# Attention scores by four products: the queries' rest against the rounded keys alone, in two 64-row tiles of TensorE

## The chip, the core and the metric

One Trainium2 chip; the kernel runs on one of its cores. The metric is the device time of one execution in microseconds; the runs of the kernel before and of the changed kernel are compared by their medians.

## What is computed

One step of a streaming encoder: an input projection, a state-space branch, a GLU, a banded attention and an output projection. The change is in the attention of the prompt's 2048 positions, 8 heads of 64 dimensions. The reference, cut to this:

```python
s = jnp.einsum('bnqhd,bnkhd->bnhqk', chunks(q), kb).astype(jnp.float32) * (HEAD_DIM ** -0.5)
bias = _rel_bias(rel_table, dist)
s = jnp.where(valid[None, :, None, None, :], s + bias[None, None], NEG_INF)
p = jax.nn.softmax(s, axis=-1).astype(v.dtype)
o = jnp.einsum('bnhqk,bnkhd->bnqhd', p, vb)
```

`q` and `k` are RMS-normalised per head. A chunk of 64 queries sees its own 64 keys and the 512 before them.

## The kernel before

TensorE multiplies values that are rounded to its fp32r format, so every number is carried as two parts: `hi`, the rounded value, and `lo`, the rest (`x - hi`, rounded again). A product of two numbers then needs several products of parts.

The program is one foreground (the input projection, then the GLU, then the output projection, all through `mm3`, lines 180 to 185: three matmuls of 512 columns for each 128 rows of the contraction) into which a background is woven (the state-space branch, the decode attention, then `attention`, lines 1093 to 1325). `run` (line 1517) adds up the costs that the foreground yields, multiplies them by `ratio`, and lets the background go on until its own yielded costs are paid. The order of all instructions is thus fixed when the program is built. It doesn't look at times, only at the yielded numbers and at counters.

**Keys and queries** are made in the input projection (`ev_norm`, lines 263 to 310). `turn` transposes a tile of 128 positions into PSUM (`pt`, 128 partitions = 2 heads x 64 dimensions, 4 pairs of heads, 128 positions). ScalarE writes `hi` (line 297), VectorE `lo` (line 298), both into `o[:, m, x, t]` with x = 0 for `hi` and 1 for `lo`. Two DMAs store `o` into the DRAM tensor `kt_d` (keys) or `qt_d` (queries).

**Scores.** `attention` goes through 16 units (a group `G` of 512 queries and a pair of heads `m`), each with 2 heads `s` and 4 blocks `a` of 128 queries: 128 steps. A unit loads keys into `KS[n]`: partitions 0 to 63 hold `hi` of a key's 64 dimensions, partitions 64 to 127 hold `lo` of the same key. `Q[n, 0]` holds the queries' `hi` twice, on both halves of the partitions, and `Q[n, 1]` their `lo` twice. So one matmul over 128 partitions adds q_hi k_hi + q_hi k_lo, and a second one q_lo k_hi + q_lo k_lo. `qk` (lines 1155 to 1176) does this over the `w` keys that the block sees: 640 keys in two halves of 320 (two PSUM banks, so four matmuls, 96 of the steps), and in the first group (`G` = 0, 32 of the steps) 128, 256, 384 or 512 keys in one bank by two matmuls. The PSUM tile `s` exists once; the next `qk` waits until it has been read.

```python
for x2 in range(2):
    nc.tensor.matmul(ps_s[:, bank, 0:wp], Q[n, x2][:, s, 128 * a:128 * a + 128],
                     KS[n][:, s, c0:c0 + wp], start=(x2 == 0), stop=(x2 == 1))
```

VectorE then adds the bias and takes each row's minimum in one instruction (line 1174; signs are turned, so the minimum serves the softmax), `soft` takes the exponential on ScalarE (line 1183), `tr` transposes the result by up to five TensorE transposes (line 1194), which ScalarE and VectorE split again into `pth` and `ptl` (lines 1201, 1202), and `pv` multiplies by the values (line 1212). A step is `qk` of block i, then foreground, then `tr` of block i - 1, then foreground, then `soft` of block i.

Elsewhere the kernel already uses parts of TensorE's array: the decode attention places matmuls in column tiles of 32 (lines 1009, 1012, 1051), and the state-space branch has transposes of 16 partitions (line 727), which the program places in a row tile of 32 rows and 128 columns. The transposes of line 1035 are placed in a tile of 128 rows and 32 columns.

Of the kernel before, what the change touches and what calls it, by code (L numbers as in the profile page):

```python
# [7 lines left out]
F32 = mybir.dt.float32  # L8
F32R = mybir.dt.float32r
I32 = mybir.dt.int32  # L10
AF = mybir.ActivationFunctionType
OP = mybir.AluOpType
# [19 lines left out]
def fv(ap):  # L32
    return ap.bitcast(F32)


def ap_of(t, offset, pat):
    return bass.AP(tensor=t.tensor, offset=t.offset + offset, ap=pat)


class Build:  # L40
# [146 lines left out]
    def inproj(self):  # L187
        nc, I, tc = self.nc, self.I, self.tc
        wp, hp, ev = self.wp, self.hp, self.ev
# [47 lines left out]
        def store(n, dst, src):  # L237
            self.defer(n, lambda: nc.sync.dma_start(dst, src))
# [24 lines left out]
        def ev_norm(g, t, z):  # L263
            r = self.rstd[:, t:t + 1]
            zs = ev.tile([128, 512], F32, tag="zs", name="zs")
            sq = ev.tile([128, 512], F32, tag="sq", name="sq", bufs=1)
            s8 = ev.tile([128, 8], F32, tag="s8", name="s8")
            nc.scalar.activation(out=sq, in_=z, func=AF.Square, scale=r)
            nc.scalar.activation(out=zs, in_=z, func=AF.Copy, scale=r)
            z3 = zs.rearrange("p (h d) -> p h d", h=8)  # L270

            def power():
                nc.vector.tensor_reduce(s8, sq.rearrange("p (h d) -> p h d", h=8), axis=AX.X, op=OP.add)  # L273
                nc.gpsimd.tensor_scalar(s8, s8, 1.0 / 64, EPS, op0=OP.mult, op1=OP.add)  # L274
                nc.gpsimd.tensor_tensor(out=s8, in0=s8, in1=self.nhalf, op=OP.pow)  # L275

            def scale():
                nc.vector.tensor_mul(z3, z3, s8[:, :, None].to_broadcast([128, 8, 64]))
                if g == "k" and t >= 12:
                    o = ev.tile([128, 512], F32, tag="plain", name="plain")  # L280
                    nc.gpsimd.tensor_tensor(out=o.rearrange("p (h d) -> p h d", h=8), in0=z3,
                                            in1=self.kgrow[:, None, :].to_broadcast([128, 8, 64]), op=OP.mult)
                    store(4, self.O["kp"][(t - 12) * 128:(t - 11) * 128] if t < 16 else self.O["ks"], o)

            def turn():
                pt = self.pst.tile([128, 4, 128], F32, tag="tr", name="pt")
                for m in range(4):
                    nc.tensor.transpose(pt[:, m], zs[:, m * 128:(m + 1) * 128], self.ident)  # L288
                gcol = (self.kg2 if g == "k" else self.qg2)[:, 0:1]
                o = ev.tile([128, 4, 2, 128], F32R, tag="kt", name="kt", bufs=1)  # L290
                if t == 16:
                    o = fv(o).rearrange("p m x t -> p (m x t)")[:, 0:512].rearrange("p (m t) -> p m t", m=4)
                    nc.scalar.activation(out=o, in_=pt, func=AF.Copy, scale=gcol)
                    store(2, self.ksd if g == "k" else self.qsd, o)
                    return
                hi, lo = o[:, :, 0], o[:, :, 1]
                nc.scalar.activation(out=hi, in_=pt, func=AF.Copy, scale=gcol)
                self.defer(2, lambda: nc.vector.scalar_tensor_tensor(lo, pt, gcol, fv(hi), op0=OP.mult,
                                                                     op1=OP.subtract))
                for h in range(2):  # L300
                    if g == "k":
                        dst = ap_of(self.kt_d, 2048 * h + 128 * t, [[4096, 64], [64 * 4096, 8], [1, 128]])
                    else:
                        dst = ap_of(self.qt_d, 64 * 1024 * (t // 4) + 512 * h + 128 * (t % 4),
                                    [[1024, 64], [4 * 64 * 1024, 8], [1, 128]])
                    store(4 + h, dst, fv(o)[64 * h:64 * h + 64].rearrange("p m x t -> p (m x) t"))

            self.defer(2, power)
            self.defer(self.T_SCALE, scale)
            self.defer(self.T_TURN, turn)  # L310

        def ev_silu(g, t, z):
# [29 lines left out]
        n = 0  # L342
# [39 lines left out]
        for ps in range(3):  # L382
            for ti, t in enumerate(TILES):
# [5 lines left out]
                for gi in range(2):  # L389
                    g = passes[ps][gi]  # L390
# [702 lines left out]
    def attention(self):  # L1093
        nc = self.nc
        st = ExitStack()
        p = self.pool(st, "att", side="right", bufs=2)
        ps = self.pool(st, "attps", side="right", space=PSUM)
        KS, Q, VB, BI, GA = {}, {}, {}, {}, {}
# [51 lines left out]
        def span(x):  # L1150

            n, s, a = x
            return a if units[n][1] else 4

        def qk(x):
            n, s, a = x
            j0 = span(x)
            w = (a + 5 - j0) * 128
            parts = [(0, w)] if w <= 512 else [(0, 320), (320, 320)]
            ps_s = ps.tile([128, 2, 512], F32, tag="s", name="s")  # L1160
            for bank, (c, wp) in enumerate(parts):
                c0 = 128 * j0 + c
                for x2 in range(2):
                    nc.tensor.matmul(ps_s[:, bank, 0:wp], Q[n, x2][:, s, 128 * a:128 * a + 128],  # L1164
                                     KS[n][:, s, c0:c0 + wp], start=(x2 == 0), stop=(x2 == 1))
            sn = p.tile([128, 640], F32, tag="sn", name="sn")
            mn = p.tile([128, 1], F32, tag="mn", name="mn")
            b = BI[2 * n + s][:, 640 - w:640]
            if len(parts) == 2:
                o, i0, i1 = (sn.rearrange("p (a k) -> p a k", a=2), ps_s[:, :, 0:320],  # L1170
                             b.rearrange("p (a k) -> p a k", a=2))
            else:
                o, i0, i1 = sn[:, 0:w], ps_s[:, 0, 0:w], b
            nc.vector.tensor_tensor_reduce(out=o, in0=i0, in1=i1, scale=1.0, scalar=3e38, op0=OP.add, op1=OP.min,  # L1174
                                           accum_out=mn)
            S[x] = sn, mn, w

        def soft(x):
# [93 lines left out]
        for i in range(N + 6):  # L1272
            self.att_left = N + 6 - i
            if i < N:
                x = subs[i]
                while not self.flags.get(("ga", 4 * units[x[0]][1] + 3)):
                    yield None
                qk(x)
                yield self.W_QT * SL
                flush()  # L1280
            done = i >= 2 and subs[i - 2][2] == 3 if i - 2 < N else False
            if done:
                n, s, a = subs[i - 2]
# [28 lines left out]
            if i < N:  # L1312
                n, r = x[0], i % 8
# [287 lines left out]
```

## Time and profile before

| | |
|---|---|
| median of 3 runs | 1228.08 us (1226.01 to 1228.82) |
| the profiled execution's own time | 1228.56 us |
| its span, first to last instruction | 1226.8 us |
| TensorE matmul busy | 1195.7 us (97%) |
| VectorE, ScalarE, GpSimd busy | 742.5, 598.2, 365.5 us |
| the score matmuls (line 1164), 448 of them | 87.5 us busy |
| VectorE's bias and minimum (line 1174), 128 of them | 93.3 us busy |

The matmul column of the profile counts an instruction from its start to its modelled end, and the next one starts before that end. So what a matmul takes in a stream is read from start to start, or from the chain that ended last, which follows ends. The weight load of a matmul (PEld) is an instruction of its own.

### The profile page before, as it was taken

The page shows a single profiled execution, that of the slowest core. Times are in us where ns is not written, and L with a number is a line of the kernel's source. Part 1 is how long each engine was busy: PE and PEld are TensorE (multiplying, and loading weights), DVE is VectorE, ACT ScalarE, POOL GpSimd, SP SyncE. Part 2 cuts the span into 40 slices and gives each one's busy share as a digit, 9 for nine tenths or more (in the row PEclk, how much of TensorE's full clock was granted, in tenths as well). Part 3 has the DMA queues.
Part 4 walks back from the last instruction along what each step waited for, and adds up shares of the span by engine and source line. Part 5 has one row for each costly group of instructions (what it writes and reads, how often), then busy time and mean ns, then how long its engine had stood idle before and what let it go on. Part 6 is the DMA issues. An engine that isn't in the chain of part 4 may idle for free.

```text
span 1226.8 us, 18936 instructions
## 1 busy us (share of the span) xinstructions
PE 1195.7 (97%) x6687; PEld 986.6 (80%) x6687; DVE 742.5 (61%) x1391; ACT 598.2 (49%) x1159; POOL 365.5 (30%) x455
## 2 busy tenths in 40 slices
PE   8999999999999998999999999999999999999998
PEld 6788888778788876887777878888888888888876
DVE  5233565968999898985444455565565555555511
ACT  6344355356666657553232356565554454554410
POOL 2432243457777645540000011111112121121120
PEclk9899999999999999999999999999999999999999
DMA  8776556655555557433895688886877778767242
GB/s 253 230 225 203 175 160 204 203 143 137 135 141 135 153 155 233 125 101 88 257 379 184 194 245 243 257 274 195 219 206 225 210 228 248 205 203 225 66 149 100
DMA packets 190119, 236.58 MB, mean 193 GB/s; under 512 B 58136, under 2 KB 122656, under 8 KB 189000
## 3 DMA queue, kind: packets, MB, share of 16 engines
q1 hardware_dynamic: 189016, 232.15, 63.3%
q0 software_dynamic: 864, 3.21, 0.9%
q8 instruction: 53, 0.87, 0.3%
q14 instruction: 42, 0.34, 0.1%
q10 hardware_dynamic: 144, 0.00, 0.0%
HBM read 169.48 MB, written 67.80 MB: 193 GB/s over the span
## 4 chain that ended last, share of the span: by engine, by line
PE 77%; DVE 6%; DMA 6%; ACT 3%; POOL 3%; issue 2%; SPq 1%; DVEq 0%; ACTq 0%; POOLq 0%
PE z L183 18%; PE z L185 18%; PE z L184 18%; PE o L1212 6%; PE pt L1194 5%; PE s L1164 5%; DMA wraw<-in_w_in_dram 3%; PE pt L288 1%; PE o L1051 1%; PE y L837 1%; PE y L836 1%; SPq L695 1%; PE v L765 1%; POOL s L275 1%; ACT whi L149 1%
## 5 line engine op out<-in xcount | busy, mean ns | idle before, releaser
L183 PE MATMUL z<-whi,hhi 128*128 128x512 f32 x816 | 340.1, 417 | 4.5 <-ACT hhi L222 2.8
L184 PE MATMUL z<-wlo,hhi 128*128 128x512 f32 x816 | 321.9, 395 | 2.0 <-DVE wlo L150 1.8
L185 PE MATMUL z<-whi,hlo 128*128 128x512 f32 x816 | 321.5, 394 | 0.0
L183 PEld LDWEIGHTS z<-whi,hhi 128*128 128x128 f32 x816 | 154.7, 190 | 41.5 <-issue 5.1
L184 PEld LDWEIGHTS z<-wlo,hhi 128*128 128x128 f32 x816 | 155.1, 190 | 34.8 <-DVE wlo L150 6.3
L185 PEld LDWEIGHTS z<-whi,hlo 128*128 128x128 f32 x816 | 154.5, 189 | 34.3 <-DVE hlo L225 0.8
L1201 ACT ACTIVATE pth<-pt 128x640 fp32r<-128x640 f32 (+4 forms) x128 | 81.8, 639 | 128.9 <-PE pt L1194 89.4
L1202 DVE TENSOR_TENSOR ptl<-pt,pth 128x640 fp32r<-128x640 f32 (+4 forms) x128 | 94.6, 739 | 60.8 <-ACT pth L1201 59.9
L183 PE MATMUL z<-whi,mh 128*128 128x512 f32 x272 | 113.7, 418 | 0.0
L1109 POOL MEMSET bias<- 64x64 f32 x32 | 4.7, 146 | 360.0 <-DMA bias<-tl_d 248.8
L1183 ACT ACTIVATE sn<-sn,mn 128x640 f32<-128x640 f32 (+4 forms) x128 | 97.0, 758 | 29.4 <-DVE mn L1174 29.4
L185 PE MATMUL z<-whi,ml 128*128 128x512 f32 x272 | 107.1, 394 | 0.5 <-POOL ml L1409 0.5
L184 PE MATMUL z<-wlo,mh 128*128 128x512 f32 x272 | 106.7, 392 | 0.0
L1174 DVE CUSTOM_DVE_ANT_0 sn<-s,bias 128x640 f32<-128x640 f32 (+4 forms) x128 | 93.3, 729 | 11.0 <-PE s L1164 10.5
L1164 PE MATMUL s<-ks,q 128*128 128x320 f32 (+1 forms) x448 | 87.5, 311 | 0.0
L1194 PE MATMUL pt<-ident,sn 128*128 128x128 f32 x560 | 82.9, 274 | 4.5 <-ACT sn L1183 2.4
L1164 PEld LDWEIGHTS s<-ks,q 128*128 128x128 f32 x448 | 74.7, 188 | 11.1 <-DVE mn L1174 1.2
L1194 PEld LDWEIGHTS pt<-ident,sn 128*128 128x128 f32 x560 | 65.0, 140 | 23.1 <-ACT sn L1183 10.7
L225 DVE TENSOR_TENSOR hlo<-xraw,hhi 128x1024 fp32r<-128x1024 f32 x49 | 60.9, 1243 | 23.3 <-ACT hhi L222 23.2
L274 POOL TENSOR_SCALAR s<-s 128x8 f32<-128x8 f32 x34 | 14.8, 435 | 184.6 <-DVE s L273 184.0
L1222 DVE TENSOR_TENSOR ot<-o,tmp 64x512 f32<-64x512 f32 x32 | 22.0, 688 | 74.5 <-ACT tmp L1220 74.5
L275 POOL TENSOR_TENSOR s<-s,nhalf 128x8 f32<-128x8 f32 x34 | 61.0, 1795 | 2.9
(268 smaller groups left out, 2165.6 us busy)
## 6 DMA issues: line engine op xcount, KB each, us to landing
xraw<-in_xT_dram SPq DMA_DIRECT2D x49, 512.0 KB, 4.2
q<-qt_d SPq DMA_DIRECT2D x64, 256.0 KB, 9.6
ks<-kt_d SPq DMA_DIRECT2D x28, 512.0 KB, 5.2
vhl<-vp_d SPq DMA_DIRECT2D x28, 512.0 KB, 6.6
wraw<-in_w_in_dram SPq DMA_DIRECT2D x48, 256.0 KB, 4.1
bias<-tl_d SPq DMA_DIRECT2D x32, 320.0 KB, 6.1
mt<-mt_d SPq DMA_DIRECT2D x17, 512.0 KB, 6.4
x<-in_x_dram SPq DMA_DIRECT2D x34, 256.0 KB, 5.6
```

Source lines behind the costliest of these rows:

```text
L183: mm(z, a, whi, start=first, stop=False)
L184: mm(z, a, wlo, start=False, stop=False)
L185: mm(z, b, whi, start=False, stop=last)
L225: nc.vector.tensor_sub(lo, raw, fv(hi))
L275: nc.gpsimd.tensor_tensor(out=s8, in0=s8, in1=self.nhalf, op=OP.pow)
L1164: nc.tensor.matmul(ps_s[:, bank, 0:wp], Q[n, x2][:, s, 128 * a:128 * a + 128], KS[n][:, s, c0:c0 + wp], start=(x2 == 0), stop=(x2 == 1))
L1174: nc.vector.tensor_tensor_reduce(out=o, in0=i0, in1=i1, scale=1.0, scalar=3e38, op0=OP.add, op1=OP.min, accum_out=mn)
L1183: nc.scalar.activation(out=sn[:, 0:w], in_=sn[:, 0:w], func=AF.Exp, scale=-1.0, bias=mn, accum_out=SUM[n][:, a, s:s + 1])
L1194: nc.tensor.transpose(t[:, k], pr[:, 128 * k:128 * k + 128], self.ident)
L1201: nc.scalar.activation(out=h, in_=t[:, 0:w], func=AF.Copy)
L1202: post.append(lambda: nc.vector.tensor_tensor(out=l, in0=t[:, 0:w], in1=fv(h), op=OP.subtract))
L1212: nc.tensor.matmul(o[:, a0:a1], VB[n][:, j, s, :], t[:, 3 * a0 + j + a0:4 * (a1 - 1) + j + 1:4], start=(y == 0 and j == 4), stop=(y == 1 a ...
```

## The change

`qk` leaves out the product q_lo k_lo. It multiplies q_hi by all 128 partitions of the keys as before, and q_lo by the 64 partitions that hold k_hi. To have two such half products at once, the keys are stacked differently: of every 128 keys, the first 64 have `hi` on partitions 0 to 63 and `lo` on 64 to 127, and the other 64 the other way round. The first kind (y = 0) goes to PSUM bank 0, the second (y = 1) to bank 1. The two half products use row tiles at row 0 and at row 64, 128 columns wide. The bias and the minimum are now one VectorE instruction for each bank, and the second starts from the first one's minimum. In `turn`, ScalarE writes the new layout in one instruction, and VectorE writes the keys' `lo` in two.

```diff
+                if g == "k":
+                    o4 = o.rearrange("p m x (y t) -> p m (x y) t", y=2)
+                    hi, lo, src = o4[:, :, 0::3], o4[:, :, 2:0:-1], pt.rearrange("p m (y t) -> p m y t", y=2)
+                nc.scalar.activation(out=hi, in_=src, func=AF.Copy, scale=gcol)
+                for y in ((0, 1) if g == "k" else (slice(0, 128),)):
+                    self.defer(2, lambda y=y: nc.vector.scalar_tensor_tensor(
+                        lo[:, :, y], src[:, :, y], gcol, fv(hi[:, :, y]), op0=OP.mult, op1=OP.subtract))
...
-            parts = [(0, w)] if w <= 512 else [(0, 320), (320, 320)]
-            for bank, (c, wp) in enumerate(parts):
-                c0 = 128 * j0 + c
-                for x2 in range(2):
-                    nc.tensor.matmul(ps_s[:, bank, 0:wp], Q[n, x2][:, s, 128 * a:128 * a + 128],
-                                     KS[n][:, s, c0:c0 + wp], start=(x2 == 0), stop=(x2 == 1))
+            q0, q1 = (Q[n, x2][:, s, 128 * a:128 * a + 128] for x2 in range(2))
+            ks = KS[n][:, s, 128 * j0:128 * j0 + w].rearrange("p (j y t) -> p y j t", y=2, t=64)
+            for y in range(2):
+                nc.tensor.matmul(ps_s[:, y, 0:w // 2], q0, ks[:, y], start=True, stop=False)
+            for y in range(2):
+                r = slice(64 * y, 64 * y + 64)
+                nc.tensor.matmul(ps_s[:, y, 0:w // 2], q1[r], ks[r, y], start=False, stop=True,
+                                 tile_position=(64 * y, 0))
...
-            nc.vector.tensor_tensor_reduce(out=o, in0=i0, in1=i1, scale=1.0, scalar=3e38, op0=OP.add, op1=OP.min,
-                                           accum_out=mn)
+            m = 3e38
+            for y in range(2):
+                nc.vector.tensor_tensor_reduce(out=o[:, y], in0=ps_s[:, y, 0:w // 2].rearrange("p (j t) -> p j t", t=64),
+                                               in1=i1[:, y], scale=1.0, scalar=m, op0=OP.add, op1=OP.min,
+                                               accum_out=mn[:, y:y + 1])
+                m = mn[:, 0:1]
+            mn = mn[:, 1:2]
```

On TensorE, in a step of 640 keys in the second half of the attention (`z` is the foreground's output projection, `s` the scores, `ks` the keys, `q` the two parts of the queries), there stood before:

```order
L184 MATMUL z<-wlo,mh 128x512
L185 MATMUL z<-whi,ml 128x512
L1164 MATMUL s<-ks,q_10225 128x320
L1164 MATMUL s<-ks,q_10259 128x320
L1164 MATMUL s<-ks,q_10225 128x320
L1164 MATMUL s<-ks,q_10259 128x320
L183 MATMUL z<-whi,mh 128x512
L184 MATMUL z<-wlo,mh 128x512
```

and now:

```order
L184 MATMUL z<-wlo,mh 128x512
L185 MATMUL z<-whi,ml 128x512
L1171 MATMUL s<-ks,q_10072 128x320 x2
L1174 MATMUL s<-ks,q_10105 128x320 x2
L183 MATMUL z<-whi,mh 128x512
L184 MATMUL z<-wlo,mh 128x512
```

Four matmuls stay four (line 1174's two are the row tiles), and what surrounds them is the same; steps of 128 to 512 keys have four now and had two. On VectorE, in a step of 640 keys while the GLU is the foreground (`ptl` is the split of an earlier block's weights, `ms` a GLU output, `mo` the gated attention output), there stood before:

```order
L1202 TENSOR_TENSOR ptl<-pt,pth 128x640
L1174 ISA sn,mn<-s,bias 128x640
L1174 ISA mn 128x1
L1391 SCALAR_TENSOR_TENSOR ms<-th,z 128x512
L1247 TENSOR_TENSOR mo<-ot,pt 128x256
```

and now:

```order
L1213 TENSOR_TENSOR ptl<-pt,pth 128x640
L1182 ISA sn,mn<-s,bias 128x5x64
L1182 ISA mn 128x1
L1182 ISA sn,mn<-s,bias,mn 128x5x64
L1182 ISA mn 128x1
L1402 SCALAR_TENSOR_TENSOR ms<-th,z 128x512
L1258 TENSOR_TENSOR mo<-ot,pt 128x256
```

One instruction with its reading of the accumulator became two, at the same place; the second reads what the first wrote.

## Rows read from the trace of the kernel before

**Rows 1.** The page: span, busy time by engine, engines on the chain.
```profile
span 1226.8 us, 18936 instructions
...
PE 77%; DVE 6%; DMA 6%; ACT 3%; POOL 3%; issue 2%; SPq 1%; DVEq 0%; ACTq 0%; POOLq 0%
```
**Rows 2.** Waits of PE, 700 to 1165 us: total us, times, longest.
```profile
PE pt L1194 <- ACT sn L1183: 2.4, 4, 1.6
PE pt L1194 <- DVE ptl L1202: 2.1, 5, 0.8
```
**Rows 3.** Windows: busy us (instructions) of PE, PEld, DVE, ACT, POOL; clock, DMA.
```profile
900.00:1000.00 100.00, 100.00 (x587) 87.30 (x586) 55.56 (x109) 51.05 (x95) 17.77 (x21) 1.00 0.73 215
```
**Rows 4.** Chain that ended last, 1048 to 1050.2 us: start, us, what.
```profile
1049.01 0.58 PE s L1164 x4
1049.59 0.23 PE z L183
```
**Rows 5.** Timeline of PE, 1048.7 to 1049.7 us: start, us, engine, line.
```profile
1048.62 0.39 PE L185 MATMUL z<-whi,ml 128*128 128x512 f32 x1
```
**Rows 6.** Timeline of PEld, the same stretch.
```profile
1048.62 0.70 PEld L1164 LDWEIGHTS s<-ks,q 128*128 128x128 f32 x4
1049.28 0.19 PEld L183 LDWEIGHTS z<-whi,mh 128*128 128x128 f32 x1
```
**Rows 7.** Timeline of PE, 259.2 to 260.4 us, around transposes in row tiles.
```profile
259.06 0.40 PE L185 MATMUL z<-whi,hlo 128*128 128x512 f32 x1
259.38 0.42 PE L727 MATMUL ut<-ident,P 16*128 16x16 f32 x4
259.73 0.50 PE L183 MATMUL z<-whi,hhi 128*128 128x512 f32 x1
260.07 0.39 PE L184 MATMUL z<-wlo,hhi 128*128 128x512 f32 x1
```
**Rows 8.** Timeline of PEld, the same stretch.
```profile
259.38 0.32 PEld L727 LDWEIGHTS ut<-ident,P 16*128 16x128 f32 x4 [0.36 <-ACT P L713]
259.73 0.19 PEld L183 LDWEIGHTS z<-whi,hhi 128*128 128x128 f32 x1
259.84 0.19 PEld L184 LDWEIGHTS z<-wlo,hhi 128*128 128x128 f32 x1
```
**Rows 9.** Timeline of PE, 638.4 to 640.4 us, around column tiles.
```profile
638.38 0.40 PE L185 MATMUL z<-whi,hlo 128*128 128x512 f32 x1
638.71 1.07 PE L1009 MATMUL s<-kc,qbd 128*32 128x264 f32 x16
639.60 0.23 PE L1012 MATMUL s<-kts,qbd 128*32 128x16 f32 x8
639.76 0.50 PE L183 MATMUL z<-whi,hhi 128*128 128x512 f32 x1
640.09 0.40 PE L184 MATMUL z<-wlo,hhi 128*128 128x512 f32 x1
```
**Rows 10.** Chain, 711 to 730 us: score matmuls of 128, 256, 384, 512 keys.
```profile
712.32 0.17 PE s L1164 x2
712.49 0.28 PE z L183
...
713.93 0.23 PE s L1164 x2
...
715.67 0.36 PE s L1164 x2
...
729.76 0.46 PE s L1164 x2
```
**Rows 11.** Groups by form on DVE, 700 to 1170 us: busy us, mean ns.
```profile
L1174 DVE CUSTOM_DVE_ANT_0 sn<-s,bias 128x640 f32<-128x640 f32 x96 | 77.9, 811 | 4.0 <-PE s L1164 3.7 <-DVE ptl L1202 0.2
L1174 DVE DVE_READ_ACCUMULATOR2_ANT mn<- 128x1 f32 x128 | 10.6, 83 | 0.0
...
L1174 DVE CUSTOM_DVE_ANT_0 sn<-s,bias 128x128 f32<-128x128 f32 x8 | 2.3, 284 | 0.7 <-PE s L1164 0.7
```
**Rows 12.** Waits of PE, whole span: the longest.
```profile
PE pt L288 <- DVE zs L278: 6.0, 4, 2.3
```
**Rows 13.** Timeline of PE, 633.9 to 634.8 us, a transpose into a column tile.
```profile
633.75 0.60 PE L1034 MATMUL pt<-ident,pr 128*128 128x128 f32 x4
634.19 0.27 PE L1035 MATMUL pt<-ident,pr 128*16 128x128 f32 x1
```

More of the change, by code (lines that the diff above doesn't have):

```diff
@@ L295, in turn @@
                     return
[L296 to L299, printed above, removed]
+                hi, lo, src = o[:, :, 0], o[:, :, 1], pt
+                if g == "k":
[5 more added lines that the diff above has]
+                        lo[:, :, y], src[:, :, y], gcol, fv(hi[:, :, y]), op0=OP.mult, op1=OP.subtract))
                 for h in range(2):
@@ L1158, in qk @@
             w = (a + 5 - j0) * 128
-            parts = [(0, w)] if w <= 512 else [(0, 320), (320, 320)]
             ps_s = ps.tile([128, 2, 512], F32, tag="s", name="s")
-            for bank, (c, wp) in enumerate(parts):
-                c0 = 128 * j0 + c
-                for x2 in range(2):
-                    nc.tensor.matmul(ps_s[:, bank, 0:wp], Q[n, x2][:, s, 128 * a:128 * a + 128],
-                                     KS[n][:, s, c0:c0 + wp], start=(x2 == 0), stop=(x2 == 1))
+            q0, q1 = (Q[n, x2][:, s, 128 * a:128 * a + 128] for x2 in range(2))
[6 more added lines that the diff above has]
+                                 tile_position=(64 * y, 0))
             sn = p.tile([128, 640], F32, tag="sn", name="sn")
-            mn = p.tile([128, 1], F32, tag="mn", name="mn")
+            mn = p.tile([128, 2], F32, tag="mn", name="mn")
             b = BI[2 * n + s][:, 640 - w:640]
[L1169 to L1173, printed above, removed]
-            nc.vector.tensor_tensor_reduce(out=o, in0=i0, in1=i1, scale=1.0, scalar=3e38, op0=OP.add, op1=OP.min,
-                                           accum_out=mn)
+            o, i1 = (v.rearrange("p (j y t) -> p y j t", y=2, t=64) for v in (sn[:, 0:w], b))
+            m = 3e38
[5 more added lines that the diff above has]
+            mn = mn[:, 1:2]
             S[x] = sn, mn, w
```

## The prediction

> **What bounds the kernel now.** The page comes first: its chain of waits. Of the chain that ended last, 77% is TensorE and no other engine has over 6%; the span is 1226.8 us [rows 1]. Next the stage that the change touches, about 711 to 1160 us. The windows view shows TensorE busy in all of 100 us of it, VectorE in 55.56 and ScalarE in 51.05 [rows 3]. The waits of TensorE there are small: it waited 2.4 us for the exponential and 2.1 us for `ptl` [rows 2]. So a nanosecond more or less on TensorE's queue in a step is a nanosecond of the end, 128 times, and work added to VectorE is covered at first. What a matmul takes is read from the chain, which follows ends: four score matmuls of 320 columns take 0.58 us, 0.145 each, and one foreground matmul of 512 columns 0.23 [rows 4]. These prices hold only while weight loads are hidden: the load of the first score matmul starts at 1048.62 us, together with the foreground matmul ahead of it, and the next one's load at 1049.28, before the last score matmul has ended [rows 5, 6].
>
> **What the change saves.** For 640 keys (96 steps) TensorE had four matmuls of 320 columns. It now has two over the whole array and two in row tiles. If the two tiles stream together, that is the time of three: 0.145 us saved a step. That tiles can run together is shown for column tiles: sixteen matmuls of 248 to 264 columns end within 1.07 us, where at 0.45 ns a column (0.145 us by 320) one after the other would need some 1.8 us in a single pass [rows 9]. For row tiles no row shows it; I take it as so, and keep the other end for the range.
>
> **What a trip into row tiles costs.** One place of the old kernel goes into row tiles and back: the transposes of 16 partitions at line 727.
> - Entry. The foreground matmul starts at 259.06 us, the first tile at 259.38: 0.32 us instead of 0.23, so 0.09 more [rows 4, 7]. The tile's weight load also starts only at 259.38 [rows 8], with its matmul and not ahead of it: nothing was loaded while the array finished. The profile names a ScalarE wait for that load, but the column tiles, without such a wait, enter as late: 638.38 to 638.71, 0.33 us [rows 9].
> - A load in the open. Behind the tiles, line 183's load starts together with its matmul at 259.73, and the next load only at 259.84, 0.11 us later; the next matmul starts 0.34 us after line 183's instead of 0.23 [rows 7, 8]. So a load of 128 columns that is not hidden costs 0.11. The row tiles of the change have 128 columns too, so I charge 0.11 on entry and 0.11 on exit. On entry the nearest row below is the column tile's 32 columns, a quarter of it.
> - Exit. The last tile of line 727 starts at about 259.59 (four of them end at 259.80, and one lasts 0.21), line 183's load at 259.73: 0.14, of which some 0.03 are its own streaming. With column tiles it is 639.65 to 639.76, 0.11 [rows 9]. I take 0.09 over the normal distance.
>
> Together 0.09 + 0.11 + 0.09 + 0.11 = 0.40 us a trip, and each of the 128 steps makes one trip, since foreground and transposes of the whole array stand on both sides of every step.
>
> **A rule against the change.** The Trainium skill ("TensorEngine Tiling (Array Packing)", Key Properties) says that changing the tiling mode drains TensorE. It has no price for it and names no load in the open; a drain alone would be 0.18 us of the 0.40. One row here goes against it: the transpose at line 1035, which the program puts into a tile of 32 columns, follows four whole-array transposes at their own spacing (633.75 and 634.19: 0.11 each) [rows 13]. So a change of tile is not always paid for; the rows of lines 727 and 1009 are nearer to the change, one in rows, the other with a tile position written out.
>
> **The sum.**
> 1. 96 steps of 640 keys: 0.40 - 0.145 = +0.255 us each, **+24.5 us**.
> 2. 32 steps of the first group. Two matmuls of 128, 256, 384, 512 columns took 0.22 (0.17 and the 0.05 by which line 183 behind it is longer), 0.23, 0.36 and 0.46, mean 0.32 [rows 10]. Now two of half the columns over the whole array, which can't be quicker than their loads, 0.11 each, so 0.22; one pair of tiles of 160 columns on average, 0.08; and the trip, 0.40. Together 0.70: +0.38 each, **+12.2 us**.
> 3. VectorE's bias and minimum. 640 columns take 811 ns, 128 take 284, so a column 1.03 ns; 320 take about 482. Two such with two readings of the accumulator at 83 ns make 1130, against 894 [rows 11]: +0.24 us a step, 30 us over all on an engine that is free for over 40% of the stage [rows 3]. On TensorE **0**: `soft` is placed behind the `tr` that follows, and each `qk` is now longer, which gives VectorE more time. Without that cover it is the fourth rival.
> 4. The keys' `lo` in two pieces: 16 more instructions, each one fixed cost of some 0.15 us (284 less 128 x 1.03), in a stage where TensorE waited 6.0 us in 4 places for VectorE ahead of `turn` [rows 12]. Bound 0 to 0.6 us, taken as **0**. ScalarE's write and the DMAs keep their number and size.
> 5. TensorE's waits of 4.5 us for `soft` and `ptl` [rows 2] get shorter when TensorE itself comes later: **-2 us**, bounds 0 and -4.5.
>
> 24.5 + 12.2 - 2 = +34.7 us. The profiled execution took 1228.6 us, so 1263.3; the median of the runs is 0.5 below it: **1263 us**.
>
> **Rivals.**
> - *The tiles take turns* (16%): the second tile's load waits for the first's, or it streams behind it, 0.11 to 0.145 us more a step, x 128 = 14 to 18 us: about 1279. For it: the two whole-array loads behind line 727's trip are 0.11 us apart [rows 8]. Against it: column tiles start together [rows 9].
> - *The trip is only a drain* (7%): the loads are hidden all the same, 0.18 instead of 0.40 a trip: 34.7 less 0.22 x 128 = 28 us, so +7, 1235. Against it: line 183's load in the open is there behind both kinds of tiles, 0.34 us to line 184 at 259.73 [rows 7] and 0.33 at 639.76 [rows 9].
> - *No trip is paid* (9%): this is the faster side. Entry and exit run through as at line 1035 [rows 13], loads go ahead, and both tiles stream at once: 96 x 0.145 = 13.9 us saved. The first group gains nothing, as its loads bind it (0.22 and 0.08 to 0.19 for the pair, against 0.32: -0.02 to +0.09 us in 32 steps, up to +3 in all). 1228 - 14 = 1214, or up to 1217. It decides at a trip of 0.145 us: below that the change gains on 640 keys. The Trainium skill ("TensorE: Matmul & The Clock Gate", Part 3, The mechanism) has loads pulled ahead where row groups don't conflict, and tiles some 4 ns apart; by that rule alone this rival is the outcome. No row here shows it for row tiles, and line 727 shows loads that weren't pulled ahead.
> - *VectorE becomes late* (5%): the second piece holds the exponential behind it in each of the 32 steps in which `pv` lies between, 0.24 to 0.3 us: up to 10 us more, 1273. Against it: rows 2 and 3.
> - *Nothing to see* (3%): a trip of just the saved 0.145 us, 1228.
>
> **How the numbers follow.** The forecast itself has 60%. A measurement of this kernel tells about 0.2% from no change, 2.5 us. Faster: 9%, the third rival. Same: 3%. Slower: 60 + 16 + 7 + 5 = 88%. The forecast's own bounds are 1250 (the entry load at a quarter, 0.08 less a trip, so -10.5 us, and -2.5 of item 5) to 1268 (item 5 at 0, +2; item 4, +0.6; 0.02 more on exit, the column tiles' 0.11, +2.6). The range goes down to 1240 and up to 1284, so that it takes in the tiles in turns and late VectorE work, and leaves out no trip, no change and most of the drain alone, 9 + 3 + 6 = 18%.
>
> **What would show it.** In a step of 640 keys TensorE's timeline should have the two matmuls of line 1171 at 0.145 us from each other, then a first row tile some 0.23 to 0.25 us after the second, with its load starting beside it, the other tile right beside it, and line 183 some 0.24 us later with its own load beside it and 0.34 us to line 184. In the chain such a step's score matmuls with their trip should take 0.84 us (0.58 + 0.255) instead of 0.58. TensorE's share of the chain stays; waits for line 1194 don't grow. Wrong would be: loads of line 1174 that start with the matmul ahead of them (then no trip is paid), tiles 0.11 us or more apart (turns), or waits of lines 1194 and 1212 for VectorE of several us (late VectorE).

## Result and profile after

| | before | changed |
|---|---|---|
| median of the compared runs | 1228.45 us (4 runs) | 1258.31 us (1256.12 to 1259.57, 4 runs) |
| ratio to before, 95% interval | | 1.024 (1.0224 to 1.0256) |
| span of the profiled execution | 1226.8 us | 1257.8 us |
| TensorE, VectorE, ScalarE busy | 1195.7, 742.5, 598.2 us | 1230.7, 772.6, 597.7 us |

The change made the kernel slower by 30 us. 1263 us was forecast, with a range of 1240 to 1284. The page of the changed kernel, its span and its chain by engine:

```profile
span 1257.8 us, 19355 instructions
...
PE 83%; DMA 7%; DVE 4%; ACT 3%; SPq 2%; issue 1%; POOL 0%; DVEq 0%; ACTq 0%; POOLq 0%
```

TensorE's share of the chain rose from 77% [rows 1] to 83%, where the forecast had it stay. The place itself, in a step of 640 keys, in the timeline of PE (start, length in us, engine, line):

```profile
1079.09 0.39 PE L185 MATMUL z<-whi,ml 128*128 128x512 f32 x1
1079.32 0.45 PE L1171 MATMUL s<-ks,q 128*128 128x320 f32 x2
1079.70 0.42 PE L1174 MATMUL s<-ks,q 64*128 64x320 f32 x2
1080.05 0.50 PE L183 MATMUL z<-whi,mh 128*128 128x512 f32 x1
1080.39 0.40 PE L184 MATMUL z<-wlo,mh 128*128 128x512 f32 x1
```

and of the weight loads, the same stretch:

```profile
1079.70 0.19 PEld L1174 LDWEIGHTS s<-ks,q 64*128 64x128 f32 x2 [0.19 <-issue]
1080.05 0.19 PEld L183 LDWEIGHTS z<-whi,mh 128*128 128x128 f32 x1 [0.16 <-issue]
1080.16 0.19 PEld L184 LDWEIGHTS z<-wlo,mh 128*128 128x128 f32 x1
```

Each part of the forecast trip is there. The two tiles load and start together: two loads lie within 0.19 us, and one load lasts 0.18; over the 96 steps the two matmuls start 3 ns apart (median). Their load starts with them at 1079.70 and not ahead of them, 0.24 us after the second matmul of line 1171, which alone would be followed after 0.145. Line 183's load starts with its matmul at 1080.05, the next load 0.11 us later, and line 184 follows 0.34 us after line 183 instead of 0.23. This is what [rows 7 to 9] showed for other tiles. In the chain (start, us, what) the step now reads:

```profile
1079.48 0.29 PE s L1171 x2
1079.77 0.35 PE s L1174 x2
1080.12 0.43 PE z L183
1080.55 0.23 PE z L184
```

0.29 + 0.35 and the 0.20 by which line 183 is longer make 0.84 us, where [rows 4] had 0.58. A step of the first group with 128 keys:

```profile
713.86 0.39 PE L185 MATMUL z<-whi,yl 128*128 128x512 f32 x1
714.10 0.30 PE L1171 MATMUL s<-ks,q 128*128 128x64 f32 x2
714.33 0.30 PE L1174 MATMUL s<-ks,q 64*128 64x64 f32 x2
714.56 0.50 PE L183 MATMUL z<-whi,yh 128*128 128x512 f32 x1
714.89 0.39 PE L184 MATMUL z<-wlo,yh 128*128 128x512 f32 x1
```

1.03 us from line 185 to line 184. From the starts of all places with line 185 ahead of the scores and lines 183 and 184 behind them (85 of the 96 steps, 6 of each 8), line 185 to line 184, the medians are:

| keys | steps | before, us | changed, us | more |
|---|---|---|---|---|
| 640 | 96 | 1.046 | 1.297 | 0.251 |
| 512 | 8 | 0.938 | 1.208 | 0.270 |
| 384 | 8 | 0.805 | 1.142 | 0.337 |
| 256 | 8 | 0.702 | 1.091 | 0.388 |
| 128 | 8 | 0.685 | 1.031 | 0.346 |

96 x 0.251 = 24.1 us and 8 x 1.341 = 10.7 us, 34.8 us in all. Against that stand TensorE's shorter waits. Its waits in the attention, total us, times, longest:

```profile
PE pt L1205 <- ACT sn L1194: 0.8, 1, 0.8
PE ty L1349 <- DMA y<-y_d: 0.6, 1, 0.6
PE pt L1205 <- DVE mn L1182: 0.6, 1, 0.6
PE pt L1205 <- DVE ptl L1213: 0.3, 1, 0.3
```

2.3 us, where before the two of [rows 2] had 4.5 and two more 2.1, 6.6 in all. 34.8 - 4.3 = 30.5 us, and the spans differ by 31.0.

VectorE's two pieces, by form (busy us, mean ns):

```profile
L1182 DVE CUSTOM_DVE_ANT_1 sn<-s,bias,mn 128x320 f32<-128x320 f32 x96 | 52.9, 551 | 5.5
L1182 DVE CUSTOM_DVE_ANT_1 sn<-s,bias 128x320 f32<-128x320 f32 x96 | 45.9, 478 | 4.7 <-PE s L1174 4.0 <-POOL bias L1114 0.6
L1182 DVE DVE_READ_ACCUMULATOR2_ANT mn<- 128x1 f32 x256 | 21.3, 83 | 0.0
```

Summed as in the forecast that is 478 + 551 + 2 x 83 = 1195 ns against 894 [rows 11]. But each reading of the accumulator starts some 75 ns before its reduction ends, so the sum counts a part twice: line 1182 is busy for 123.3 us in all, where line 1174 was for 94.3, so 29 us more or 0.23 a step.

### The profile page after: what moved, and what is told of

The parts are those of the page before. It is cut to its first block, busy times and chain, and to the rows that moved or that the text cites. A ratio compares the mean times of both kernels' runs of the same rounds, so it can differ in the third digit from the quotient of the medians.

```text
span 1257.8 us, 19355 instructions
## 1 busy us (share of the span) xinstructions
PE 1230.7 (98%) x6751; PEld 986.6 (78%) x6751; DVE 772.6 (61%) x1663; ACT 597.7 (48%) x1159; POOL 364.4 (29%) x455
## 4 chain that ended last, share of the span: by engine, by line
PE 83%; DMA 7%; DVE 4%; ACT 3%; SPq 2%; issue 1%; POOL 0%; DVEq 0%; ACTq 0%; POOLq 0%
PE z L183 21%; PE z L185 19%; PE z L184 19%; PE o L1223 5%; PE pt L1205 5%; PE s L1174 3%; DMA wraw<-in_w_in_dram 3%; PE s L1171 3%; PE pt L288 1%; PE v L770 1%; PE o L1056 1%; PE y L842 1%; PE y L841 1%; PE ut L732 1%; DMA kc<-in_kcT_dram 1%
## 5 line engine op out<-in xcount | busy, mean ns | idle before, releaser
L184 PEld LDWEIGHTS z<-wlo,hhi 128*128 128x128 f32 x816 | 155.3, 190 | 34.8 <-DVE wlo L150 6.1
L185 PEld LDWEIGHTS z<-whi,hlo 128*128 128x128 f32 x816 | 154.7, 190 | 34.8 <-DVE hlo L225 1.0
L183 PE MATMUL z<-whi,mh 128*128 128x512 f32 x272 | 121.5, 447 | 0.0
L1182 DVE CUSTOM_DVE_ANT_1 sn<-s,bias,mn 128x320 f32<-128x320 f32 (+3 forms) x120 | 62.9, 524 | 6.3
L183 PEld LDWEIGHTS z<-whi,mh 128*128 128x128 f32 x272 | 51.1, 188 | 16.2 <-issue 11.7
L183 PE MATMUL z<-whi,yh 128*128 128x512 f32 x136 | 63.7, 469 | 0.0
```

The lines of the kernel that those rows point to most:

```text
L183: mm(z, a, whi, start=first, stop=False)
L184: mm(z, a, wlo, start=False, stop=False)
L185: mm(z, b, whi, start=False, stop=last)
L1182: nc.vector.tensor_tensor_reduce(out=o[:, y], in0=ps_s[:, y, 0:w // 2].rearrange("p (j t) -> p j t", t=64), in1=i1[:, y], scale=1.0, scala ...
```

## Experiments

**The rest over the whole array.** The changed kernel, line 1174 without tiles:

```diff
-                r = slice(64 * y, 64 * y + 64)
-                nc.tensor.matmul(ps_s[:, y, 0:w // 2], q1[r], ks[r, y], start=False, stop=True,
-                                 tile_position=(64 * y, 0))
+                nc.tensor.matmul(ps_s[:, y, 0:w // 2], q1, ks[:, y], start=False, stop=True)
```

> The changed kernel with its new stacking of the keys and its two VectorE instructions, but with the queries' rest over all 128 partitions of the array (it adds the product of the two rests again), so that no row tile is left. Theory (the loss is the trip into row tiles and back): a step of 640 keys costs what it did before, 0.58 us; the first group's steps have four matmuls that their weight loads bind at 0.11 us, 0.45 us on average instead of 0.32, +4 us in 32 steps; so 1230 to 1234 us, against 1228 before and 1258 changed. Rival (VectorE's second piece or the new stacking carries part of the loss): clearly over 1236, up to 1258.

1231.12 us against 1226.10, ratio 1.0049 (1.003 to 1.0068), as expected. The chain has the score matmuls back at 0.58 us, with nothing longer behind them:

```profile
1001.30 0.29 PE s L1171 x2
1001.59 0.29 PE s L1173 x2
1001.88 0.23 PE z L183
```

So 25 of the 30 us go with the tiles alone; the new stacking and VectorE's second piece stayed in this kernel. Of the 5 us that are left, 4.3 are the first group's four matmuls, from the starts as in the table above. VectorE's second piece shows here too: in seven steps the first score matmul starts 0.28 to 0.58 us after line 185 instead of 0.23, 0.11 to 0.16 us after VectorE's second piece, which reads the one PSUM tile `s`, has ended. That is 1.8 us; waits ahead of the transposes are 0.5 us shorter. In the changed kernel only four steps start late, by 0.3 us together.

**One tile, in turn.** The kernel before, with the rest in one row tile:

```diff
-                for x2 in range(2):
-                    nc.tensor.matmul(ps_s[:, bank, 0:wp], Q[n, x2][:, s, 128 * a:128 * a + 128],
-                                     KS[n][:, s, c0:c0 + wp], start=(x2 == 0), stop=(x2 == 1))
+                nc.tensor.matmul(ps_s[:, bank, 0:wp], Q[n, 0][:, s, 128 * a:128 * a + 128],
+                                 KS[n][:, s, c0:c0 + wp], start=True, stop=False)
+            for bank, (c, wp) in enumerate(parts):
+                c0 = 128 * j0 + c
+                nc.tensor.matmul(ps_s[:, bank, 0:wp], Q[n, 1][0:64, s, 128 * a:128 * a + 128],
+                                 KS[n][0:64, s, c0:c0 + wp], start=False, stop=True, tile_position=(0, 0))
```

> The kernel before, with its stacking and its one VectorE instruction, but with the queries' rest against the rounded keys alone in one row tile, rows 0 to 63, for both banks: the two tile matmuls must take turns. Theory (one trip of about 0.40 us a step, and the two tiles of the change do run at once): 0.14 us more than the changed kernel in each of 96 steps, about as much as it in the first group, so 1258 + 14 = about 1272 us. Rival (the change's two tiles don't really overlap, or VectorE's second piece costs time): at or below 1258.

1268.58 us, ratio 1.0348 (1.0322 to 1.0374): 42.5 us more than before, 12.6 more than the change cost, where 14 was expected (1272 us). The chain:

```profile
1003.22 0.29 PE s L1163 x2
1003.51 0.49 PE s L1167 x2
1004.00 0.43 PE z L183
```

The two tile matmuls take 0.49 us here and 0.35 in the changed kernel. The difference, 0.14, is one matmul of 320 columns. So the change's tiles do run at once, and the saving that it was to bring is real; the trip costs more. The second tile's load doesn't add to it: it starts 0.11 us behind the first one's, while the first tile's matmul is still under way (1003.55, and the second matmul starts at 1003.69). From the first tile to line 183 there are 0.49 us (1003.44 to 1003.93 in its timeline), 0.11 of open load, two matmuls and the drain.

**Two trips a step.** The changed kernel, with whole array and tile in turns (the two loops over `y` made one).

> The changed kernel with its four matmuls in another order: whole array, row tile, whole array, row tile, so two trips a step and never two tiles at once. Theory (each trip pays its drains and open loads anew): +0.54 us in 96 steps and +0.42 to 0.55 in 32, some 67 us in all, 1325 us. Rival (the cost is paid once a step, or by the tiles' own streaming): +0.14 us a step, about 1276.

1317.78 us, ratio 1.0745 (1.0715 to 1.0775): 91.7 us over before, 62 more than the change with its one trip; 67 was expected (1325 us), 18 by the rival. The timeline of PE, one step:

```profile
1002.75 0.30 PE L1172 MATMUL s<-ks,q 128*128 128x320 f32 x1
1002.98 0.41 PE L1173 MATMUL s<-ks,q 64*128 64x320 f32 x1
1003.33 0.41 PE L1172 MATMUL s<-ks,q 128*128 128x320 f32 x1
1003.67 0.41 PE L1173 MATMUL s<-ks,q 64*128 64x320 f32 x1
1004.00 0.50 PE L183 MATMUL z<-whi,mh 128*128 128x512 f32 x1
1004.34 0.39 PE L184 MATMUL z<-wlo,mh 128*128 128x512 f32 x1
```

From the first whole-array matmul to the first tile there are 0.23 us, 0.145 for the matmul and 0.09 for the drain, as its own load lay ahead of it. From there to line 183 there are 0.34 us between any two: 0.145 for the matmul, 0.11 for its load and 0.09 for the drain. Each change of tile is paid for anew, in both directions alike.

**A tiny trip added to the kernel before.** Behind the score matmuls, one row-tile matmul of 64 columns that nothing reads:

```diff
+            nc.tensor.matmul(ps_s[:, 1, 320:384], Q[n, 1][0:64, s, 128 * a:128 * a + 128],
+                             KS[n][0:64, s, 128 * j0:128 * j0 + 64], start=True, stop=True, tile_position=(0, 0))
```

> The kernel before, with one row-tile matmul of 64 columns added behind each step's score matmuls; it writes to a part of the scores' second bank that nothing reads. It measures the trip by itself: drain 0.09, open load 0.11, 0.03 of streaming, drain 0.10, open load 0.11, so 0.42 us a step or 54 us in all 128, less 2 to 4 us that TensorE no longer waits: 1278 to 1281. Rival (a trip is cheap, and the change loses its time elsewhere): under 1245, where 128 x 0.03 us of streaming and a load of 0.11 would be 1246.

1273.06 us, ratio 1.0387 (1.0355 to 1.0419), 43 to 51 us more than before. The chain:

```profile
1005.92 0.58 PE s L1164 x4
1006.51 0.23 PE s L1166
1006.73 0.43 PE z L183
```

0.23 + 0.20 = 0.43 us for a matmul that streams 64 columns. The time lies below the expected 1278 to 1281, and far from the rival's 1245. From the starts, as in the table above, the trip is 0.42 us in 96 steps and 0.40 on average in 32, 53 us, as expected. What was off is TensorE's waits: from start to start the rest of the attention is 6 to 7 us shorter than before, most of it ahead of the transposes of the exponentials, where 2 to 4 us were allowed for.

**The rest over 96 rows, no tile.** As the first run, but half of the rest's matmuls take 96 partitions:

```diff
-                nc.tensor.matmul(ps_s[:, y, 0:w // 2], q1, ks[:, y], start=False, stop=True)
+                r = slice(0, 96 + 32 * y)
+                nc.tensor.matmul(ps_s[:, y, 0:w // 2], q1[r], ks[r, y], start=False, stop=True)
```

> As the run with the rest over the whole array, but the rest of the first half blocks is multiplied over 96 partitions only; the program gives it no tile position, and builds it as a matmul of the whole array. Theory (what is paid for is the change of tile, not that fewer rows than 128 take part): no wait ahead of it, its load goes ahead, and the time is that of the whole-array run, 0.4 to 0.6% over the kernel before. Rival (every matmul of other than 128 rows makes the array drain): 0.4 us a step more, some 50 us.

1231.34 us, ratio 1.0031 (1.0014 to 1.0048). The interval takes in the lower part of the expected 0.4 to 0.6%, and the rival's 50 us are far off. The timeline:

```profile
1001.78 0.39 PE L185 MATMUL z<-whi,ml 128*128 128x512 f32 x1
1002.02 0.45 PE L1171 MATMUL s<-ks,q 128*128 128x320 f32 x2
1002.30 0.47 PE L1174 MATMUL s<-ks,q 96*128 96x320 f32 x2
1002.61 0.39 PE L183 MATMUL z<-whi,mh 128*128 128x512 f32 x1
1002.84 0.39 PE L184 MATMUL z<-wlo,mh 128*128 128x512 f32 x1
```

1.06 us from line 185 to line 184, where a trip makes 1.30 and the run over the whole array 1.05. So 96 rows without a tile cost 0.01 us a step; the change of tile is what is paid for. 64 rows without a tile were not run.

**No rest at all.** The changed kernel without the loop of line 1174.

> The changed kernel without the queries' rest at all: only the two whole-array matmuls of a step stay, so the scores lack the product of the queries' rest and the keys. It shows what the rest's own streaming is worth, and whether TensorE still sets the end when a step gets shorter. Theory (TensorE's queue sets the end): two matmuls of 0.145 us less than before in 96 steps, 28 us, and some 0.09 us in 32, 3 us: 31 us less than before, of which new waits may give back up to 5: 1195 to 1200. So a trip that cost nothing would have gained at most about 14 of these. Rival (VectorE or ScalarE takes over as soon as TensorE gets shorter): over 1210.

1210.31 us against 1227.64, ratio 0.9862 (0.9845 to 0.9878): 17 us less, and 27 to 32 were expected. This theory fell: from line 185 to line 184 the steps got shorter by 31 us, and not all of it arrived at the end. The idle time ahead of the transposes, by what ended it, over the whole span (us, times; that of their weight loads and of the matmuls themselves added up), in the kernel before:

```profile
  ACT sn L1183: 13.1, 32
  DVE ptl L1202: 4.9, 18
```

and without the rest:

```profile
  ACT sn L1190: 21.1, 39
  DVE ptl L1209: 10.3, 22
```

Of the waits for the exponential, 10.7 us were the loads' before, and 18.8 are now. A load's idle time lies partly beneath the matmul ahead of it, so what was lost is read from the starts: the distances that end at such a transpose are 10 us longer than before. Another 2.1 us went in seven steps whose first score matmul starts late, 0.11 to 0.16 us after VectorE's second piece has ended.

**No rest, and VectorE's one piece.** The kernel before, with `x2` = 0 alone.

> The kernel before, with its stacking and its one VectorE instruction a step, without the queries' rest (the scores lack the product of the queries' rest and the keys). The other run without the rest, with two VectorE instructions, gained 17 us where its shorter matmuls gave back 31: TensorE waited longer ahead of the transposes of the exponentials. Theory A (VectorE's second piece, 0.24 us a step, makes the exponential late as soon as TensorE is shorter): 1200 or less here. Theory B (the chain from scores to transposes, ScalarE's two passes of it above all, is nearly as long as TensorE's own queue, with one piece or two): 1207 to 1211, as with two pieces.

1207.94 us against 1229.11, ratio 0.9822 (0.9794 to 0.9849): 21 us less, theory B. The same rows:

```profile
  ACT sn L1182: 25.8, 45
  DVE ptl L1201: 9.7, 20
```

Even with VectorE's one piece the transposes wait for the exponentials, longer than before (the loads 21.4 us, where 10.7 were). From the starts, the distances that end at such a transpose are nearly 12 us longer than before. The two runs without the rest are 4 us apart, and their intervals touch. Some 2 of the 4 aren't VectorE's: in the first group this kernel has one score matmul a step and saves 5.2 us there, where the other has two and saves 3.0, so it saves 33 us in all and not 31. The other 2 are the late first score matmuls: with one piece such delays add up to 0.1 us. Which part of the chain from the scores to the transposes makes it long was not separated. Both kernels leave out a part of the scores, so they are measurements of this limit and no better versions.

**Tiles, and VectorE's one piece.** The changed kernel, one VectorE instruction over both banks:

```diff
...
-            for y in range(2):
-                nc.vector.tensor_tensor_reduce(out=o[:, y], in0=ps_s[:, y, 0:w // 2].rearrange("p (j t) -> p j t", t=64),
...
+            o, i1 = (v.rearrange("p (y k) -> p y k", y=2) for v in (sn[:, 0:w], b))
+            nc.vector.tensor_tensor_reduce(out=o, in0=ps_s[:, :, 0:w // 2], in1=i1, scale=1.0, scalar=3e38, op0=OP.add, op1=OP.min,
+                                           accum_out=mn[:, 0:1])
...
```

> The changed kernel with its row tiles, but bias and minimum in one VectorE instruction a step over both banks, in the banks' order (so the biases meet other keys, and the weights other values: the output differs, the amount of work of all other instructions doesn't). Theory (with the trips in the way TensorE's queue sets the end, and VectorE's second piece is hidden): 1257 to 1259, as the changed kernel. Rival (the second piece is part of the loss): 128 x 0.24 us at most, down to 1228 + 5; anything under 1254 would show it.

1255.27 us against 1229.11, ratio 1.0199 (1.0171 to 1.0227). That is 2 us under the expected band and above the 1254 that would have spoken for the rival; by the median alone it is not clear. The trace tells more. The first and the last score matmul of the changed kernel (first and last start):

```profile
L1171 PE MATMUL s<-ks,q x256: 191/305/394, 714.1 to 1190.1; 128*128 128x320 f32 x96, 128*128 128x64 f32 x8, 128*128 128x128 f32 x8, 128*128 128x192 f32 x8
```

and with one piece:

```profile
L1171 PE MATMUL s<-ks,q x256: 191/305/394, 712.7 to 1187.9; 128*128 128x320 f32 x96, 128*128 128x64 f32 x8, 128*128 128x128 f32 x8, 128*128 128x192 f32 x8
```

476.0 us against 475.2: the second piece is worth under 1 us of the attention. The two profiled spans are 2.2 us apart (1257.8 and 1255.6 us); the other 1.4 us lie ahead of the attention, where the two kernels are the same.

## Why the prediction was right, and where it was off

- **The bound.** TensorE's queue set the end, and the trip's 0.40 us landed on it step by step. That held in the direction of the change: made longer by 0.25 to 0.78 us a step of 640 keys, TensorE's time came out at the end but for 4 to 7 us of shorter waits. It doesn't hold the other way (the runs without the rest): of 31 us less on TensorE 17 arrived, of 33 us 21. So the third rival, no trip paid, was priced too fast. By these shares some 8 to 9 of its 14 us would have arrived, about 1220 us and not 1214; that is an estimate, as no run made the steps shorter by 14 us. In the sentence "a nanosecond more or less on TensorE's queue in a step is a nanosecond of the end", the word "less" is what failed. [rows 2] show only waits that outlast the modelled end of a matmul, 2.4 us for the exponential, while the loads had already waited 10.7 us for it.
- **The trip.** Forecast 0.09 + 0.11 + 0.09 + 0.11 from the transposes of line 727 and the column tiles. Measured in the same pieces by the run with one tile, from start to start: 0.239 instead of 0.147 on entry (0.092), 0.253 instead of 0.147 to the second tile (0.106), 0.235 instead of 0.146 on exit (0.089), 0.338 instead of 0.230 to line 184 (0.108): 0.395 us.
- **Two at once.** Taken from column tiles, true for row tiles: 3 ns apart. The rival with tiles in turn was built as a kernel of its own and costs 12.6 us more.
- **The sum.** Item 1 +24.5, measured 24.1. Item 2 +12.2, measured 10.7: a step took 0.65 us and not 0.70. The tile's load is in the open here too, and paid in full: the tiles of 64 columns start 0.22 us ahead of line 183, 0.03 of streaming and the 0.11 and 0.09 of the forecast. What was charged too high is the two whole-array matmuls, 0.22 by two loads and 0.09 of drain: from the first one's start to the first tile there are 0.28 us on average, as the first one's load lies beneath line 185. Item 3, VectorE: 30 us more forecast for the bias and the minimum, 29 measured, and under 1 us at the end. That this is so near is in part luck: 83 ns for a reading counts an overlap twice, and the second piece takes 551 ns and not 482, for which nobody waited in the changed kernel. Item 5: -2, and TensorE's listed waits fell by 4.3. Together 1263 forecast, 1258 measured: most of the 5 us are items 2 and 5.
- **The rule.** In the steps of 640 keys, entry into a row tile and exit from it each cost 0.09 us over the normal distance, and the first load behind each change stood in the open, 0.106 to 0.108 us. The Trainium skill ("TensorEngine Tiling (Array Packing)", Key Properties) says that changing the tiling mode drains TensorE. The trace agrees for these tiles, but the drain alone is 0.18 of the 0.40 us. In the run with one tile the second tile's load starts ahead of its matmul; at both changes of mode the load starts only with its matmul. The Trainium skill ("TensorE: Matmul & The Clock Gate", Part 3, The mechanism) has loads pulled ahead of matmuls in flight. The trace agrees inside a tile mode, and not across the change.

What stays open: why the transposes into a column tile of line 1035 pay nothing [rows 13]. No run was made for it, but the trace of the kernel before narrows it. Line 923, a transpose into 32 columns without a written tile position, doesn't pay either: it starts 0.24 us after line 185, and line 183 0.03 us after it. The column tiles with a written position (lines 680, 843, 1009, 1051) start 0.32 to 0.33 us after line 185 (medians). So few columns alone are not what is paid for. A trip shared by several steps wasn't tried. At 0.145 us saved and 0.40 a trip it would by this sum take three steps of 640 keys to gain, with six PSUM banks of scores; the kernel has room for two.

## What to carry to other kernels

Before a matmul goes into a part of the array, look for a place in the trace that already does so, and read four distances there: the last whole-array matmul to the first tile, the first tile's load, the last tile to the next load, and that load. Here they came to 0.40 us a round trip, so tiles pay only if one trip saves more than that, some 900 columns of streaming at 0.45 ns. And a saving on the engine that bounds the end is to be checked against the chain that comes next: here 14 of 31 us, and 12 of 33, taken from TensorE didn't arrive.

## What was not expected

- Over a third of the time taken from TensorE didn't arrive at the end; most of it went into waits ahead of the transposes of the exponentials, though the page has TensorE busy in 97% of the span and [rows 2] list 4.5 us. Waits shorter than what the modelled end of a matmul covers don't show as idle time of TensorE; the starts show them.
- A step with a matmul of 96 partitions without a tile takes 0.01 us more than one with 128, with no drain; one of 64 columns in a row tile takes 0.43 us.
- The VectorE reduction that starts from a per-row minimum takes 551 ns where the one that starts from a constant takes 478. In the first group it is the same at every width, 61 to 81 ns from 64 to 256 columns. The two also read different PSUM banks, so what makes the difference was not separated.
